# A transformer layer on one core: Ada sums beside the next part's rows, a fifth PSUM bank for the mLSTM scores, and the order of columns at the first boundary

## The chip, the cores and the metric

The kernel runs on one core of a Trainium2 chip. The metric is the device time of one execution in microseconds (us). Engines are named as in the profile: PE (TensorE, matmuls), DVE (VectorE), ACT (ScalarE), POOL (GpSimd), SP (SyncE, here only a queue of DMA issues).

## What is computed

One layer on x of 256 x 2048 in fp32, with a condition vector c of 2048 values. Cut to what matters:

```python
ada = silu(c) @ w_ada + b_ada                 # 2048 x 18432
sh1, sc1, g1, sh2, sc2, g2, sh3, sc3, g3 = split(ada, 9)
h = swiglu(modulate(x, sh1, sc1), ffn1_w_in, ffn1_w_out)
x = layernorm(ALPHA * x + 0.5 * (1 + g1) * h)
h = token_mixer(modulate(x, sh2, sc2), w_in, ..., w_out)
x = layernorm(ALPHA * x + (1 + g2) * h)
h = swiglu(modulate(x, sh3, sc3), ffn2_w_in, ffn2_w_out)
x = layernorm(ALPHA * x + 0.5 * (1 + g3) * h)
```

`modulate` is a layer norm, times 1 + scale, plus shift. The token mixer multiplies by `w_in` and runs eight heads of causal softmax attention with forget gates (fox) and four mLSTM heads (q and k through a short convolution, then for each head scores q k times a decay, times v, divided by a norm), gates the result and multiplies by `w_out`.

## The kernel before

All matmuls with weights take each fp32 weight tile apart into a high and a low part and add three products: high weight with high x, low weight with high x, high weight with low x (lines 369, 370, 371). For a weight tile `raw` that SP loads (1 MB, line 344), ACT writes `hi` (a cast, line 142) and DVE writes `lo` = raw - hi (line 143). A lo tile is named after its use: `lo_fv512_12` is the third of unit 1 of the columns fv.

The stages in time: the start (the first Ada values), the first feed-forward part, boundary 1 (layer norm, modulation, first columns of the mixer), the mixer (columns named mo, fv512, mv512, mv0, m0, m1, fb, fbk, fa, fak, fv0, with attention and mLSTM heads among them), the out-projection (`o_mx`, weights mxo), boundary 2, the second feed-forward part, the end.

**The Ada queue.** Most of `silu(c) @ w_ada` is summed in the background on DVE. A part is 1024 columns: 16 rows of 128 x 1024, each loaded by SP into `ar` (two buffers) and added as `acc += ar * silu(c)` (lines 155 and 157). A row is called ar6_0_7: vector 6, part 0, row 7. Then the part's end: the sum over the 128 partitions, by a split of acc into `ahi` and `alo`, two matmuls with ones into a bank `bc`, and either a diagonal product `dg` and a reduction (pairs of shift and scale) or an addition into `gate`. The queue is one generator. `pump(n)` adds n to what is owed (R_MX a step in the mixer) and takes that many rows; a PAUSE inside a part's end stops it until the next step, so no row of the next part stands beside the end of one. `need(n)` runs the queue on until n vectors are done. Rows are pinned: they stay on DVE where they were recorded.

**PSUM.** Eight banks: a ring `mm` of five for the large products, a ring `aux` of three for all small ones: transposes `tp`, `bc`, and for each mLSTM head `gb` (the gate row over the partitions, and the second score block), `sps` (the first score block) and `nps` (two: numerator and norm). DVE turns sps and gb into `dm` (lines 1264, 1265), PE multiplies dm with v into nps (1271), DVE makes `dn` from nps (1276 to 1279), ACT scales nps into yM (1280) and squares into nps (1281).

**Boundaries.** `boundary` modulates pairs of 128-column blocks: ACT or DVE writes the normed `n` (312), PE transposes it into tp (316), ACT and DVE write the modulated columns `xf` (326, 323), then ACT and DVE split it into `xhi`, `xlo` (332, 334). For boundary 1 there are eight pairs; the later ones are written beside the first mixer products.

What sets the order: the framework's scheduler puts each engine's instructions in order by its own estimate, except where `manual_schedule` or a pin keeps the order of the code. Every engine then takes its own queue strictly in order.

Of the kernel before, what the change touches and what calls it, by code (L numbers as in the profile page):

```python
# [7 lines left out]
F32 = mybir.dt.float32  # L8
# [6 lines left out]
P = 128  # L15
# [17 lines left out]
def layer_kernel(  # L33
# [30 lines left out]
    def mm_tile(name):  # L64
        return pm.tile([P, 512], F32, tag="mm", name=name)

# [105 lines left out]

    def ada_pair(v, js):
        for j in js:
            src = pair_cols(v, j)
            acc = ap.tile([P, 2, 512], F32, tag="acc", name=f"acc{v}_{j}")
            for k in range(KD):
                raw = ap.tile([P, 2, 512], F32, tag="araw", bufs=2, name=f"ar{v}_{j}_{k}")
                SP.dma_start(raw, src[k * P:(k + 1) * P])
                ada_acc(acc, raw, k)  # L180
                yield
            for i in range(2):
                parts = ada_split(acc[:, i, :], f"{v}_{j}_{i}")
                for _ in range(2):
                    yield PAUSE
                bc = ada_sum(parts, f"{v}_{j}_{i}")
                dg = ap.tile([P, 4, P], F32, tag="alo", name=f"dg{v}_{j}_{i}")
                V.tensor_tensor(out=dg, in0=bc.rearrange("p (a b) -> p a b", b=P),
                                in1=ident.unsqueeze(1).to_broadcast([P, 4, P]), op=ALU.mult)
                V.tensor_reduce(out=scsh[:, v + i, j * 4:(j + 1) * 4], in_=dg, axis=AX.X, op=ALU.add)  # L190
            cs = scsh[:, v:v + 2, j * 4:(j + 1) * 4]
            V.tensor_tensor(out=cs, in0=cs, in1=bcol[:, v:v + 2, j * 4:(j + 1) * 4], op=ALU.add)

    def ada_gate(v, s):
        for j in range(2):
            c0 = v * D + j * 1024
            acc = ap.tile([P, 1024], F32, tag="acc", name=f"acc{v}_{j}")
            for k in range(KD):
                raw = ap.tile([P, 1024], F32, tag="araw", bufs=2, name=f"ar{v}_{j}_{k}")
                SP.dma_start(raw, w_ada[0, k * P:(k + 1) * P, c0:c0 + 1024])  # L200
                ada_acc(acc, raw, k)
                yield
            for i in range(2):
                parts = ada_split(acc[:, i * 512:(i + 1) * 512], f"{v}_{j}_{i}")
                yield PAUSE
                if i == 0:
                    G_.dma_start(gate[:, j * 1024:(j + 1) * 1024], b_ada[0:1, c0:c0 + 1024].to_broadcast([P, 1024]))
                yield PAUSE
                bc = ada_sum(parts, f"{v}_{j}_{i}")
                gs = gate[:, j * 1024 + i * 512:j * 1024 + (i + 1) * 512]  # L210
                V.scalar_tensor_tensor(out=gs, in0=bc, scalar=1.0, in1=gs, op0=ALU.add, op1=ALU.add)
                if s != 1.0:
                    V.tensor_scalar_mul(gs, gs, s)

    ada_left = {}
    PAUSE = 1

    def ada_queue(*parts):
        def gen():
            for p in parts:  # L220
                yield from p
                parts_done[0] += 1
                yield PAUSE
        ada_left["g"] = gen()

    parts_done = [0]
    owed = [0]

    def pump(n):
        owed[0] += n  # L230
        while owed[0] >= 1:
            with pinned():
                got = next(ada_left["g"], 0)
            if got is PAUSE:
                break
            owed[0] -= 1


    def need(n):
        while parts_done[0] < n and next(ada_left["g"], 0) != 0:  # L240
            owed[0] = 0

# [30 lines left out]
    def ntag():  # L273
        seq[0] += 1
        return str(seq[0])
# [29 lines left out]
    def modulate_tile(v, a, k0, nk, rs, xT, xs=None, on_v=False):  # L305
        ts_ = slice(a * P, (a + 1) * P)
        n = npool.tile([P, nk * P], F32, tag="n", bufs=2, name=f"n_{ntag()}")
        r = res[:, a, k0 * P:(k0 + nk) * P]
        if on_v:
            V.tensor_scalar(out=n, in0=r, scalar1=rs[:, 2:3], scalar2=rs[:, 0:1], op0=ALU.add, op1=ALU.mult)  # L310
        else:
            S.activation(n, r, AF.Identity, bias=rs[:, 1:2], scale=rs[:, 0:1])
        tp = aux_tile(f"tp{ntag()}")
        tpv = tp.rearrange("p (k t) -> p k t", k=4)
        for q in range(nk):
            PE.transpose(tpv[:, q, :], n[:, q * P:(q + 1) * P], ident)
        yield
        xf = npool.tile([P, nk, P], F32, tag="xf" if xs is None else "xe", bufs=2 if xs is None else 6,
                        name=f"xf{ntag()}")
        for q in range(nk):  # L320
            k = k0 + q
            if q % 2 and (a or k0 >= 6):
                V.tensor_scalar(out=xf[:, q, :], in0=tpv[:, q, :], scalar1=scsh[:, v + 1, k:k + 1],
                                scalar2=scsh[:, v, k:k + 1], op0=ALU.mult, op1=ALU.add)
            else:
                S.activation(xf[:, q, :], tpv[:, q, :], AF.Identity,
                             bias=scsh[:, v, k:k + 1], scale=scsh[:, v + 1, k:k + 1])
# [238 lines left out]
    def boundary(add_up, st, lgb, v, tag, xT, entry, nk, raws):  # L566
# [16 lines left out]
        m = [[modulate_tile(v, a, k, 2, mr[a], xT, xs if k < 6 else None, a + k == 0) for k in range(0, nk, 2)]  # L583
             for a in range(2)]
        m0, m1 = m
# [50 lines left out]
        with tc.manual_schedule(engines={dve}):  # L636
            for i in range(3, len(m0)):
# [280 lines left out]
    gap(lnp, 320, "gap_h")  # L918
    need(1)
    W = w_in[0]  # L920
# [13 lines left out]
    def finish1(products, add_up, st):  # L934
        need(2)
        products(0)
# [33 lines left out]
    mow = {}  # L970
    fence, _, xs, ws = boundary(*ent["f"], lgb, 3, "1", xT, entry_of(mo_load, mow, 3, 6), KD, raws)
    lnp.release()

# [56 lines left out]

    def cols_form_b(c0, col, ws, use, name):
        ps = {(a, b): mm_tile(f"b_{name}{col}{a}{b}") for b in range(len(ws)) for a in range(2)}
        cb = [sum(ws[:b]) for b in range(len(ws) + 1)]
# [33 lines left out]
    def form_a_four(c0, name, before_last=lambda: None):  # L1067
        ps = [mm_tile(f"pr_{name}{i}") for i in range(2)]
        for u in range(4):
# [179 lines left out]
    def mlstm_head(o, h):  # L1249
# [122 lines left out]
    def before(k):  # L1372
        until([f"row{i}" for i in (k, k + 1)])
        if k == 2:
            need(4)

# [50 lines left out]
    guw = {}  # L1427
    fence, mr2, xs, ws = boundary(*ent["f"], lgb, 6, "2", xT, entry_of(gu_load, guw, 3, 4), 8, raws)
    lnp.release()

# [35 lines left out]
    for j in range(2, 10):  # L1466
# [3 lines left out]
        if j == 7:  # L1470
            mb = late_features(2, 5)
# [5 lines left out]
    mb = late_features(3, 6)  # L1477
    gups = {(a, g): mm_tile(f"gf{g}{a}") for a in range(2) for g in range(2)}
# [23 lines left out]
    ffn_in(W2, xT, hT, 10, "f2", at(R_B))  # L1502
    need(7)
    xp.release()
# [43 lines left out]
```

## Time and profile before

| | |
|---|---|
| time, median of 3 runs | 1933.53 us (1931.28 to 1937.57) |
| the profiled execution | 1933.74 us, its span 1932.0 us, mean granted clock 0.995 |
| PE busy | 1894.1 us, 98% of the span |
| DVE busy | 1485.9 us, 77% |
| ACT busy | 950.1 us, 49% |
| POOL busy | 56.4 us, 3% |
| chain that ended last | PE 83%, DMA 7%, DVE 6%, issue 2%, ACT 1% |
| moved by DMA | 510.92 MB, mean 264 GB/s |

A busy PE is modelled from pipelined matmuls: a row's duration covers its way through the array, and the next matmul starts before it ends. The share of idle time and what ended it are read from the windows and from the waits; a wait is put down to the instruction that, by the profile, came last.

### The profile page before, as it was taken

The page shows a single profiled execution, that of the slowest core. Times are in us where ns is not written, and L with a number is a line of the kernel's source. Part 1 is how long each engine was busy: PE and PEld are TensorE (multiplying, and loading weights), DVE is VectorE, ACT ScalarE, POOL GpSimd, SP SyncE. Part 2 cuts the span into 40 slices and gives each one's busy share as a digit, 9 for nine tenths or more (in the row PEclk, how much of TensorE's full clock was granted, in tenths as well). Part 3 has the DMA queues.
Part 4 walks back from the last instruction along what each step waited for, and adds up shares of the span by engine and source line. Part 5 has one row for each costly group of instructions (what it writes and reads, how often), then busy time and mean ns, then how long its engine had stood idle before and what let it go on. Part 6 is the DMA issues. An engine that isn't in the chain of part 4 may idle for free.

```text
span 1932.0 us, 32380 instructions
## 1 busy us (share of the span) xinstructions
PE 1894.1 (98%) x13133; PEld 1725.4 (89%) x13133; DVE 1485.9 (77%) x1847; ACT 950.1 (49%) x1359; POOL 56.4 (3%) x82
## 2 busy tenths in 40 slices
PE   6999999999999999999989999999999999999997
PEld 3999999999988887699989886999999999988886
DVE  6778988777778898878987888767766665555776
ACT  3554453443454554845655645555444444444562
POOL 1111100000000000100000000000000000000000
PEclk9999999999999999999999999999999999999999
DMA  9978969999898886488887894987776776655552
GB/s 356 377 260 316 327 217 307 312 310 316 289 340 290 290 304 219 153 305 305 301 295 242 300 307 165 308 292 255 250 255 226 263 239 197 233 184 193 196 194 90
DMA packets 283566, 510.92 MB, mean 264 GB/s; under 512 B 10866, under 2 KB 134418, under 8 KB 282392
## 3 DMA queue, kind: packets, MB, share of 16 engines
q1 hardware_dynamic: 275640, 480.53, 73.1%
q0 software_dynamic: 7776, 28.32, 4.2%
q8 instruction: 103, 1.69, 0.4%
q14 instruction: 47, 0.39, 0.1%
HBM read 506.71 MB, written 2.10 MB: 263 GB/s over the span
## 4 chain that ended last, share of the span: by engine, by line
PE 83%; DMA 7%; DVE 6%; issue 2%; ACT 1%; POOL 0%; SPq 0%; DVEq 0%; ACTq 0%; POOLq 0%
PE gu_f L370 8%; PE gu_f L369 8%; PE gu_f L371 8%; PE o_f L369 7%; PE o_f L371 7%; PE o_f L370 7%; PE s L369 4%; PE s L371 4%; PE s L370 4%; DMA ar<-in_w_ada_dram 4%; DVE acc L157 2%; PE fh L370 2%; PE fh L371 2%; PE fh L369 2%; PE fs L370 1%
## 5 line engine op out<-in xcount | busy, mean ns | idle before, releaser
L157 DVE SCALAR_TENSOR_TENSOR acc<-ar,csil,acc 128x1024 f32<-128x1024 f32 x242 | 307.9, 1273 | 93.6 <-DMA ar<-in_w_ada_dram 91.9
L370 PE MATMUL s<-xlo_f,hi_s 128*128 128x256 f32 x768 | 213.9, 278 | 1.1 <-DVE xlo_f L300 1.1
L369 PE MATMUL s<-xhi_f,hi_s 128*128 128x256 f32 x768 | 213.9, 279 | 0.2 <-ACT hT1a L859 0.2
L371 PE MATMUL s<-xhi_f,lo_s 128*128 128x256 f32 x768 | 213.7, 278 | 0.0
L371 PE MATMUL gu_f<-xhi_f,lo_f2i 128*128 128x256 f32 x768 | 212.3, 276 | 0.0
L369 PE MATMUL gu_f<-xhi_f,hi_f2i 128*128 128x256 f32 x768 | 212.3, 276 | 0.0
L370 PE MATMUL gu_f<-xlo_f,hi_f2i 128*128 128x256 f32 x768 | 212.3, 276 | 0.0
L143 DVE TENSOR_TENSOR lo_f2i<-raw_f2i,hi_f2i 128x1024 fp32r<-128x1024 f32 x96 | 117.5, 1225 | 88.6 <-ACT hi_f2i L142 88.6
L371 PE MATMUL gu_f<-xhi_f,lo_f1i 128*128 128x256 f32 x640 | 177.0, 277 | 0.0
L369 PE MATMUL gu_f<-xhi_f,hi_f1i 128*128 128x256 f32 x640 | 176.9, 276 | 0.0
L370 PE MATMUL gu_f<-xlo_f,hi_f1i 128*128 128x256 f32 x640 | 176.9, 276 | 0.0
L142 ACT CAST hi_f2i<-raw_f2i 128x1024 fp32r<-128x1024 f32 x96 | 100.8, 1050 | 135.2 <-PE gu_f L370 120.7
L142 ACT CAST hi_s<-raw_s 128x1024 fp32r<-128x1024 f32 x96 | 100.5, 1052 | 130.9 <-PE s L370 90.9
L370 PEld LDWEIGHTS s<-xlo_f,hi_s 128*128 128x128 f32 x768 | 145.6, 190 | 1.4 <-DVE xlo_f L300 1.4
L371 PEld LDWEIGHTS s<-xhi_f,lo_s 128*128 128x128 f32 x768 | 145.4, 189 | 0.0
L369 PEld LDWEIGHTS s<-xhi_f,hi_s 128*128 128x128 f32 x768 | 145.0, 189 | 0.4 <-ACT hT1a L859 0.4
L370 PEld LDWEIGHTS gu_f<-xlo_f,hi_f2i 128*128 128x128 f32 x768 | 144.2, 188 | 0.2
L369 PEld LDWEIGHTS gu_f<-xhi_f,hi_f2i 128*128 128x128 f32 x768 | 144.2, 188 | 0.2
L371 PEld LDWEIGHTS gu_f<-xhi_f,lo_f2i 128*128 128x128 f32 x768 | 144.2, 188 | 0.0
L143 DVE TENSOR_TENSOR lo_f2o<-raw_f2o,hi_f2o 128x1024 fp32r<-128x1024 f32 x86 | 105.3, 1224 | 43.3 <-ACT hi_f2o L142 43.3
L143 DVE TENSOR_TENSOR lo_s<-raw_s,hi_s 128x1024 fp32r<-128x1024 f32 x96 | 115.7, 1221 | 28.1 <-ACT hi_s L142 26.8
L369 PE MATMUL o_f<-hi_f1o,hh 128*128 128x512 f32 x336 | 132.2, 393 | 0.0
(476 smaller groups left out, 5402.4 us busy)
## 6 DMA issues: line engine op xcount, KB each, us to landing
ar<-in_w_ada_dram SPq DMA_DIRECT2D x227, 512.0 KB, 5.4
raw_f2i<-in_ffn_w_in_dram SPq DMA_DIRECT2D x48, 1024.0 KB, 5.1
raw_s<-in_ffn_w_in_dram SPq DMA_DIRECT2D x47, 1024.0 KB, 7.5
raw_f1o<-in_ffn_w_out_dram SPq DMA_DIRECT2D x44, 1024.0 KB, 7.5
raw_f2o<-in_ffn_w_out_dram SPq DMA_DIRECT2D x44, 1024.0 KB, 5.1
raw_f1i<-in_ffn_w_in_dram SPq DMA_DIRECT2D x40, 1024.0 KB, 7.4
ar<-in_w_ada_dram POOLq DMA_DIRECT2D x48, 512.0 KB, 6.8
raw_mxo<-in_w_out_dram SPq DMA_DIRECT2D x16, 1024.0 KB, 7.7
```

The source lines that it names most:

```text
L142: S.copy(hi, src)
L143: return V.tensor_tensor(out=lo, in0=src, in1=hi.bitcast(F32), op=ALU.subtract)
L157: V.scalar_tensor_tensor(out=acc, in0=raw, scalar=csil[:, k:k + 1], in1=acc, op0=ALU.mult, op1=ALU.add)
L369: PE.matmul(o, ah, bh, start=start, stop=False)
L370: PE.matmul(o, ah, bl, start=False, stop=False)
L371: PE.matmul(o, al, bh, start=False, stop=stop)
```

## The change

Three edits.

1. The Ada queue becomes a class. A part's end (`tail`) no longer stands in line with the rows: `pump` first takes one step of a waiting tail and then as many rows as are owed, so rows of the next part are added while the part before is being finished. Two parts are then alive at once, so parts sum alternately in the one tile `acc` and in a half of the tile `gate` (`low`, `high`), where that half isn't needed; `stage` says from which boundary on that is so. The gate's bias is loaded in two pieces of 512 columns instead of one of 1024, and `need` counts parts instead of vectors.
2. The ring `mm` gets four banks and a fifth tag `m5` takes the bank that is left. In most of the kernel `mm_tile` still goes round five. In the fox columns before the heads (`form_a_four`) and in fv0 it uses the four, and the mLSTM score tile `sps` goes into `m5` instead of the ring `aux`.
3. At boundary 1 the columns `xf` of pair i + 1 are written before the splits of pair i. `xf` gets four buffers instead of two, `xe` four instead of six.

```diff
-    pm = ctx.enter_context(tc.tile_pool(name="pm", bufs=5, space=PSUM))
+    pm = ctx.enter_context(tc.tile_pool(name="pm", bufs=1, space=PSUM))
...
+    def mm_tile(name, four=False):
+        turn[0] = 0 if four else turn[0] % 5 + 1
+        if turn[0] == 5:
+            return fifth_tile(name)
+        return pm.tile([P, 512], F32, tag="mm", bufs=4, name=name)
...
+        def row(self):
+            if self.rows is None:
+                if not self.units or self.stage < self.units[0][1]:
+                    return False
+                if self.units[0][0] is None and any(own for own, _ in self.tails):
+                    return False
+                where, _, rows, tail, shape, tag = self.units.pop(0)
+                acc = where() if where else ap.tile(shape, F32, tag="acc", name=f"acc{tag}")
...
+        def pump(self, n):
+            self.owed += n
+            with pinned():
+                if self.tails:
+                    self.tail()
+            while self.owed >= 1:
+                with pinned():
+                    if not self.row():
+                        break
+                self.owed -= 1
...
-        xf = npool.tile([P, nk, P], F32, tag="xf" if xs is None else "xe", bufs=2 if xs is None else 6,
-                        name=f"xf{ntag()}")
+        xf = npool.tile([P, nk, P], F32, tag="xf" if xs is None else "xe", bufs=4, name=f"xf{ntag()}")
...
+            columns(3)
+            for i in range(3, len(m0)):
                 if i == 3:
                     next(m1[2])
                     for b in (m0[2], m1[2]):
                         next(b)
+                if i + 1 < len(m0):
+                    columns(i + 1)
...
-        sps = [aux_tile(f"sps{h}")[:, :T], gb[:, T:T + P]]
+        sps = [fifth_tile(f"sps{h}")[:, :T], gb[:, T:T + P]]
...
-    ada_queue(ada_gate(2, 0.5), ada_pair(3, range(4)), ada_pair(6, range(2)), ada_gate(5, 1.0),
-              ada_pair(6, range(2, 3)), ada_pair(6, range(3, 4)), ada_gate(8, 0.5))
+    ada.gate(2, 0.5, None, high)
+    for j in range(4):
+        ada.pair(3, j)
+    ada.pair(6, 0)
+    ada.pair(6, 1, low, stage=1)
+    ada.gate(5, 1.0, None, high, stage=1)
+    ada.pair(6, 2)
+    ada.pair(6, 3, low, stage=2)
+    ada.gate(8, 0.5, high, None, stage=2)
...
-    cols_form_b(C_FV, 0, [512], use_fv, "fv")
+    cols_form_b(C_FV, 0, [512], use_fv, "fv", True)
```

Where it moves instructions, three places. PE at the third mLSTM head, before: from the numerator of the first head (nps01) on, with the products of the columns fbk behind gb2.

```order
L1271 MATMUL nps01_10508<-yM0_8718,dm0_10332 128x257
L1273 MATMUL nps01_10508<-yM0_8718,dm0_10332 128x257
L1257 MATMUL gb2_10524<-ng_8735,rowsel_8742 128x256
L1259 MATMUL gb2_10524<-o_2_9834 128x128
L369 MATMUL pr_fbk0_10444<-xhi_mx_8216,hi_fbk10_10540 128x256
L370 MATMUL pr_fbk0_10444<-xlo_mx_8217,hi_fbk10_10540 128x256
```

And PE there after the change.

```order
L1315 MATMUL nps01_10508<-yM0_8719,dm0_10354 128x257
L1317 MATMUL nps01_10508<-yM0_8719,dm0_10354 128x257
L1301 MATMUL gb2_10524<-ng_8736,rowsel_8743 128x256
L1303 MATMUL sps2_10525<-o_2_9834 128x256
L1303 MATMUL gb2_10524<-o_2_9834 128x128
L399 MATMUL pr_fbk0_10444<-xhi_mx_8217,hi_fbk10_10540 128x256
L400 MATMUL pr_fbk0_10444<-xlo_mx_8218,hi_fbk10_10540 128x256
```

The score product sps2 stood 21 products of fbk later and now stands between the two products into gb2; sps3 moved up by 3 in the same way.

DVE in the mixer's columns fv512, before: the lo tiles of units 1 and 2, with the Ada rows 6 and 7 of part 6_0.

```order
L143 TENSOR_TENSOR lo_fv512_11_8854<-raw_fv512_1_8835,hi_fv512_11_8853 128x520
L143 TENSOR_TENSOR lo_fv512_12_8870<-raw_fv512_1_8835,hi_fv512_12_8869 128x520
L143 TENSOR_TENSOR lo_fv512_13_8886<-raw_fv512_1_8835,hi_fv512_13_8885 128x520
L157 SCALAR_TENSOR_TENSOR acc6_0_8573<-ar6_0_6_8710,csil_94,acc6_0_8573 128x1024
L143 TENSOR_TENSOR lo_fv512_20_8907<-raw_fv512_2_8904,hi_fv512_20_8906 128x520
L157 SCALAR_TENSOR_TENSOR acc6_0_8573<-ar6_0_7_8832,csil_94,acc6_0_8573 128x1024
```

And DVE there after the change.

```order
L165 SCALAR_TENSOR_TENSOR acc6_0_8574<-ar6_0_6_8711,csil_94,acc6_0_8574 128x1024
L151 TENSOR_TENSOR lo_fv512_11_8855<-raw_fv512_1_8836,hi_fv512_11_8854 128x520
L165 SCALAR_TENSOR_TENSOR acc6_0_8574<-ar6_0_7_8833,csil_94,acc6_0_8574 128x1024
L151 TENSOR_TENSOR lo_fv512_12_8871<-raw_fv512_1_8836,hi_fv512_12_8870 128x520
L151 TENSOR_TENSOR lo_fv512_13_8887<-raw_fv512_1_8836,hi_fv512_13_8886 128x520
L151 TENSOR_TENSOR lo_fv512_20_8908<-raw_fv512_2_8905,hi_fv512_20_8907 128x520
```

Rows 6 and 7 moved up: row 7 stood behind five lo tiles of units 1 and 2 (lo_fv512_10 to _20) and now stands behind two, ahead of lo_fv512_12.

DVE at the end of the out-projection, before: the lo tiles of the last columns and rows 14 and 15 of part 6_2.

```order
L143 TENSOR_TENSOR lo_mxo1536_30_12319<-raw_mxo1536_3_12316,hi_mxo1536_30_12318 128x1024
L157 SCALAR_TENSOR_TENSOR acc6_2_12026<-ar6_2_14_12257,csil_94,acc6_2_12026 128x1024
L439 BN_STATS st_mx1_11737<-res_91 128x6
L157 SCALAR_TENSOR_TENSOR acc6_2_12026<-ar6_2_15_12296,csil_94,acc6_2_12026 128x1024
L143 TENSOR_TENSOR lo_mxo1536_31_12323<-raw_mxo1536_3_12316,hi_mxo1536_31_12322 128x1024
```

And DVE there after the change.

```order
L491 SCALAR_TENSOR_TENSOR res_91<-res_91,o_mx011_11741 128x512
L151 TENSOR_TENSOR lo_mxo1536_30_12320<-raw_mxo1536_3_12317,hi_mxo1536_30_12319 128x1024
L469 BN_STATS st_mx1_11737<-res_91 128x6
L151 TENSOR_TENSOR lo_mxo1536_31_12324<-raw_mxo1536_3_12317,hi_mxo1536_31_12323 128x1024
L151 TENSOR_TENSOR lo_mxo1536_10_12332<-raw_mxo1536_1_12329,hi_mxo1536_10_12331 128x1024
```

The two rows left this place: row 15 now stands six instructions ahead of lo_mxo1536_30, row 14 another six ahead of that.

More of the change, by code (lines that the diff above doesn't have):

```diff
@@ L171, in ada_sum @@
         return bc
[L173 to L180, printed above, removed]
-                yield
[L182 to L231, printed above, removed]
-            with pinned():
[L233 to L241, printed above, removed]
+    def ada_rows(acc, src, tag):
+        for k in range(KD):
+            raw = ap.tile(list(acc.shape), F32, tag="araw", bufs=2, name=f"ar{tag}_{k}")
+            SP.dma_start(raw, src[k * P:(k + 1) * P])
+            ada_acc(acc, raw, k)
+            yield
@@ new lines, in pair_tail @@
+    def pair_tail(acc, v, j):
+        for i in range(2):
+            parts = ada_split(acc[:, i, :], f"{v}_{j}_{i}")
+            for _ in range(2):
+                yield
+            bc = ada_sum(parts, f"{v}_{j}_{i}")
+            dg = ap.tile([P, 4, P], F32, tag="alo", name=f"dg{v}_{j}_{i}")
+            V.tensor_tensor(out=dg, in0=bc.rearrange("p (a b) -> p a b", b=P),
+                            in1=ident.unsqueeze(1).to_broadcast([P, 4, P]), op=ALU.mult)
+            V.tensor_reduce(out=scsh[:, v + i, j * 4:(j + 1) * 4], in_=dg, axis=AX.X, op=ALU.add)
+        cs = scsh[:, v:v + 2, j * 4:(j + 1) * 4]
+        V.tensor_tensor(out=cs, in0=cs, in1=bcol[:, v:v + 2, j * 4:(j + 1) * 4], op=ALU.add)
@@ new lines, in gate_tail @@
+    def gate_tail(acc, v, j, s):
+        c0 = v * D + j * 1024
+        for i in range(2):
+            parts = ada_split(acc[:, i * 512:(i + 1) * 512], f"{v}_{j}_{i}")
+            yield
+            gs = gate[:, j * 1024 + i * 512:j * 1024 + (i + 1) * 512]
+            G_.dma_start(gs, b_ada[0:1, c0 + i * 512:c0 + (i + 1) * 512].to_broadcast([P, 512]))
+            yield
+            bc = ada_sum(parts, f"{v}_{j}_{i}")
+            V.scalar_tensor_tensor(out=gs, in0=bc, scalar=1.0, in1=gs, op0=ALU.add, op1=ALU.add)
+            if s != 1.0:
+                V.tensor_scalar_mul(gs, gs, s)
@@ new lines, in layer_kernel, with __init__, pair, gate @@
+    class AdaQueue:
+        def __init__(self):
+            self.units, self.rows, self.tails = [], None, []
+            self.done = self.owed = self.left = self.stage = 0
+        def pair(self, v, j, where=None, stage=0):
+            self.units.append((where, stage, lambda acc: ada_rows(acc, pair_cols(v, j), f"{v}_{j}"),
+                               lambda acc: pair_tail(acc, v, j), [P, 2, 512], f"{v}_{j}"))
+        def gate(self, v, s, *where, stage=0):
+            for j in range(2):
+                cols = w_ada[0, :, v * D + j * 1024:v * D + (j + 1) * 1024]
+                self.units.append((where[j], stage, lambda acc, cols=cols, j=j: ada_rows(acc, cols, f"{v}_{j}"),
+                                   lambda acc, j=j: gate_tail(acc, v, j, s), [P, 1024], f"{v}_{j}"))
+        def tail(self):
+            if next(self.tails[0][1], 0) == 0:
+                self.tails.pop(0)
+                self.done += 1
+        def row(self):
[6 more added lines that the diff above has]
+                acc = where() if where else ap.tile(shape, F32, tag="acc", name=f"acc{tag}")
+                if len(shape) == 3 and where:
+                    acc = acc.rearrange("p (v n) -> p v n", v=2)
+                self.rows, self.tail_next, self.left = rows(acc), (where is None, tail(acc)), KD
+            next(self.rows)
+            self.left -= 1
+            if not self.left:
+                self.tails.append(self.tail_next)
+                self.rows = None
+            return True
+        def pump(self, n):
+            self.owed += n
+            with pinned():
+                if self.tails:
[5 more added lines that the diff above has]
+                self.owed -= 1
+        def need(self, n):
+            while self.done < n:
+                self.owed = 0
+                if self.tails:
+                    self.tail()
+                else:
+                    self.row()
@@ L245, in rsqrt @@
+    ada = AdaQueue()
+    pump, need = ada.pump, ada.need
     def rsqrt(dst, vv):
@@ L636, in boundary, with columns @@
         with tc.manual_schedule(engines={dve}):
-            for i in range(3, len(m0)):
+            def columns(i):
                 for _ in range(2):
@@ L1028, in layer_kernel, with cols_form_b @@
     emptied = [None]
[L1031 to L1032 removed]
+    def cols_form_b(c0, col, ws, use, name, four=False):
+        ps = {(a, b): mm_tile(f"b_{name}{col}{a}{b}", four) for b in range(len(ws)) for a in range(2)}
         cb = [sum(ws[:b]) for b in range(len(ws) + 1)]
@@ L1067, in form_a_four @@
     def form_a_four(c0, name, before_last=lambda: None):
-        ps = [mm_tile(f"pr_{name}{i}") for i in range(2)]
+        ps = [mm_tile(f"pr_{name}{i}", True) for i in range(2)]
         for u in range(4):
```

24 lines of the change are left out of this document (14 added, 10 removed).

## The prediction

> **What bounds the kernel now.** I read the page first, then the windows, then TensorE's waits, then the timelines of single places. The page (busy time, one costly group, one group of DMA issues):
>
> ```profile
> PE 1894.1 (98%) x13133; PEld 1725.4 (89%) x13133; DVE 1485.9 (77%) x1847; ACT 950.1 (49%) x1359; POOL 56.4 (3%) x82
> L157 DVE SCALAR_TENSOR_TENSOR acc<-ar,csil,acc 128x1024 f32<-128x1024 f32 x242 | 307.9, 1273 | 93.6 <-DMA ar<-in_w_ada_dram 91.9
> ar<-in_w_ada_dram SPq DMA_DIRECT2D x227, 512.0 KB, 5.4
> ```
>
> TensorE is busy in all but 1932.0 - 1894.1 = 37.9 us, and the change neither adds nor removes matmuls. So it can pay only where TensorE waits. The windows (length, then each engine's busy time, granted clock, DMA share, GB/s) say where that is:
>
> ```profile
> 840.00:875.00 35.00, 34.35 (x284) 33.94 (x283) 25.73 (x35) 15.07 (x29) 0.00 (x0) 1.00 0.90 310
> 875.00:970.00 95.00, 95.00 (x723) 89.84 (x722) 84.19 (x118) 59.51 (x95) 0.00 (x0) 1.00 0.87 299
> 970.00:976.00 6.00, 4.58 (x39) 4.33 (x38) 5.08 (x9) 2.94 (x7) 0.00 (x0) 1.00 0.87 303
> 988.60:992.00 3.40, 3.40 (x19) 3.40 (x18) 2.77 (x4) 0.78 (x1) 0.00 (x0) 0.50 0.93 340
> 1215.00:1900.00 685.00, 684.93 (x4939) 639.80 (x4938) 462.97 (x508) 335.40 (x432) 0.00 (x0) 1.00 0.69 231
> 1900.00:1932.00 32.00, 21.40 (x140) 19.41 (x138) 17.78 (x30) 0.26 (x1) 3.05 (x2) 0.87 0.19 66
> ```
>
> In the feed-forward parts (the second, 1215 to 1900, is shown) TensorE has no gap: whatever is reordered there is free while its cover holds, and the cover is VectorE's spare third (busy 462.97 of 685). The last window's 10.6 us tail is not touched. What can be touched lies in the mixer, and TensorE's waits name it:
>
> ```profile
> PE sps L1259 <- DVE dm L1265: 3.8, 2, 2.4
> PE o_mx L370 <- DVE lo_mxo L143: 1.9, 2, 1.3
> PE nps L1271 <- DVE dm L1265: 1.6, 1, 1.6
> PE tp L316 <- DVE xf L323: 0.8, 1, 0.8
> PE bc L170 <- DVE alo L143: 0.7, 1, 0.7
> PE o_mx L369 <- DVE res L461: 0.6, 1, 0.6
> PE b_mv L370 <- DVE lo_mv L143: 0.5, 1, 0.5
> PE o_mx L369 <- ACT yF L1086: 0.3, 1, 0.3
> PE sps L1259 <- ACT nps L1281: 0.2, 1, 0.2
> ```
>
> Those sum to 10.4 us. Sums are made against the profiled run (1933.74 us; its span 1932.0), 0.2 above the median of 1933.53. A difference of 0.3%, 5.8 us, is about what a measurement of this kernel can tell from no change.
>
> **The mLSTM heads (banks).** The timeline of TensorE at the three large waits, of the drain that frees the third, and of VectorE's products:
>
> ```profile
> 972.67 0.48 PE L1259 MATMUL sps<-o 128*128 128x256 f32 x1 [1.42 <-DVE dm L1265]
> 981.06 0.48 PE L1271 MATMUL nps<-yM,dm 128*128 128x257 f32 x1 [1.58 <-DVE dm L1265]
> 987.35 0.67 PE L1259 MATMUL sps<-o 128*128 128x256 f32 x2 [2.40 <-DVE dm L1265]
> 987.05 0.39 ACT L1281 ACTIVATE nps<-yM 128x256 f32<-128x256 f32 x1
> 972.53 0.28 DVE L1265 TENSOR_TENSOR dm<-gb,dm 128x128 f32<-128x128 f32 x1
> 972.73 2.35 DVE L143 TENSOR_TENSOR lo_fbk<-raw_fbk,hi_fbk 128x1024 fp32r<-128x1024 f32 x2
> 976.47 2.66 DVE L157 SCALAR_TENSOR_TENSOR acc<-ar,csil,acc 128x1024 f32<-128x1024 f32 x2 [1.39 <-DMA ar<-in_w_ada_dram]
> 979.05 1.22 DVE L143 TENSOR_TENSOR lo_fbk<-raw_fbk,hi_fbk 128x1024 fp32r<-128x1024 f32 x1
> 980.92 0.28 DVE L1265 TENSOR_TENSOR dm<-gb,dm 128x128 f32<-128x128 f32 x1
> ```
>
> The third wait is put down to dm, but dm1 had ended at 981.20. sps2 sits in the bank of nps00 in the ring of three, and scalar's read of nps00 ended at 987.05 + 0.39 = 987.44; with the 2.40 us went a second loss, the 988.60:992.00 row: clock 0.50 for 3.40 us, worth 1.7. Today's heads: 1.42 + 1.58 + 2.40 + 0.2 idle, 1.7 of clock: 7.3.
>
> After: sps has its own bank, so sps2's wait goes. What is late next, in order:
> (a) sps1 still needs dm0 (its bank is sps0's). VectorE gets there with five more Ada rows done (5 x 1.27 = 6.4) and one more lo (1.22): 7.6 us put into a stretch whose VectorE idle is 95.00 - 84.19 = 10.8 (875 to 970). Not all of that idle can be filled; I take dm0 1.0 later (ends 0 and 2.5): wait 2.4.
> (b) gb2 now waits for dm1, in place of nps01. From dm0's end (972.81) to dm1's (981.20) VectorE took 8.4: three lo, two acc, 1.39 of DMA wait, and dm1's own steps, 1.0. After, it has two lo and two acc: 2 x 1.22 + 2 x 1.27 + 1.0 = 6.0. TensorE needs 6.8 from sps1 to gb2's place (981.06 - 1.58 - 972.67). Wait 0.
> (c) nps10 takes the nps00 bank, 48 matmuls after gb2. The chain from dm1's end to that read is 987.44 - 981.20 = 6.2 now, and holds as many instructions after. TensorE is there some 6 us after gb2, about level; I take 0.3, and 0.3 for nps11's bank.
> (d) gb3 needs nps11's bank: 0.5 (ends 0 and 2).
> Sum 3.5; 3.5 - 7.3 = **-3.8** (ends -7.3, if nothing comes back, and -0.6, if dm0 is 1.5 later still and the low clock comes with it).
>
> The Trainium skill (TensorE: Matmul & The Clock Gate, Part 1) puts the drop to half clock after an idle window of about 3.4 us, in windows that run free of the kernel. Here it came after 2.40 us idle, so the measurement decides; by that rule the drop would not hang on this wait, and the sum would be 1.7 higher, 1931.8.
>
> **The first mixer stage: rows ahead of tiles.** Now two Ada rows stand in other places of VectorE's queue, and a row waits there for its transfer with the lo tiles behind it. VectorE at the two places, and TensorE at the first tile in question and at the mv tiles:
>
> ```profile
> 839.88 1.28 DVE L157 SCALAR_TENSOR_TENSOR acc<-ar,csil,acc 128x1024 f32<-128x1024 f32 x1 [1.95 <-DMA ar<-in_w_ada_dram]
> 840.11 0.28 PE L370 MATMUL b_fv<-lo_fv,xhi_mx 128*128 128x256 f32 x1
> 858.86 1.28 DVE L157 SCALAR_TENSOR_TENSOR acc<-ar,csil,acc 128x1024 f32<-128x1024 f32 x1 [2.83 <-DMA ar<-in_w_ada_dram]
> 860.97 0.39 PE L370 MATMUL b_mv<-lo_mv,xhi_mx 128*128 128x256 f32 x1 [0.54 <-DVE lo_mv L143]
> 872.12 0.70 DVE L143 TENSOR_TENSOR lo_mv<-raw_mv,hi_mv 128x520 fp32r<-128x520 f32 x1 [3.34 <-ACT hi_mv L142]
> ```
>
> Row 7 of that part is taken up at 839.88 because its transfer lands then; today lo_fv512_12 is ahead of it. After, it is behind: 839.88 + 1.20 + 0.70 = 841.8 against TensorE's need at 840.11: +1.7. At 858.86 the same happens with row 13, but a TensorE that is 1.7 late finds lo_mv512_10 nearly ready, and today's two losses there (0.7 and 0.3 by start-to-start times) fall into that. At 872 row 0 of the next part goes ahead of lo_mv512_30, whose hi comes late already (3.34); that row's transfer now goes out as soon as row 14 is done, near 865.5, and SP's queue holds raw_mv0_0 behind it. With the median of 5.4 it is there before the tile; with 9 it holds it by 3. I take 0.4. Sum 1.7 - 1.0 + 0.4 = **+1.1** (ends -0.5 and +4).
>
> **First boundary.** The columns of the next pair come before the current pair's splits, with four xf buffers. What goes is the tp wait (0.8 idle, 1.2 with the start-up behind it). What comes: scalar now does hi_mo_31 ahead of n171, which the second tp needs:
>
> ```profile
> 803.00 0.44 PE L316 MATMUL tp<-ident,n 128*128 128x128 f32 x2 [0.76 <-DVE xf L323]
> 799.50 0.60 ACT L312 ACTIVATE n<-res,mr 128x256 f32<-128x256 f32 x1
> 800.00 1.03 ACT L142 CAST hi_mo<-raw_mo 128x1024 fp32r<-128x1024 f32 x1
> 800.93 0.45 ACT L326 ACTIVATE xf<-tp,scsh 128x128 f32<-128x128 f32 x1
> ```
>
> n171 would start a hi_mo (1.03) and a column (0.45) later than at 799.50, so it ends at 801.6; TensorE comes to that tp 2.5 us, eleven 512-wide matmuls (0.23 each, below), before the 803.00 row: +1.1, plus 0.3 for n175 in the same way. Net about +0.2, which falls into the wait at 840, whose end a transfer sets: **0** (ends -1.2 and +1).
>
> **fv0 and out-projection.** TensorE at the first o_mx tiles:
>
> ```profile
> 1088.06 0.39 PE L369 MATMUL o_mx<-hi_mxo,yh 128*128 128x512 f32 x1
> 1089.22 0.39 PE L371 MATMUL o_mx<-hi_mxo,yl 128*128 128x512 f32 x1
> ```
>
> Five matmuls on is 1.16 us, 0.23 each. fv0's four outputs now lie in the four rotating banks, so the o_mx tile that waits for yF's copy (0.3 above) is the second instead of the fourth: six matmuls sooner, 1.4. **+1.3** (ends 0 and 1.4). The o_mx wait for res gets an Ada row between its two steps: **+0.6** (ends 0, 1.2). At the end rows 14 and 15 no longer stand between lo_mxo1536_30 and _31:
>
> ```profile
> 1162.48 1.28 DVE L157 SCALAR_TENSOR_TENSOR acc<-ar,csil,acc 128x1024 f32<-128x1024 f32 x1 [2.63 <-DMA ar<-in_w_ada_dram]
> 1166.75 0.50 PE L370 MATMUL o_mx<-lo_mxo,yh 128*128 128x512 f32 x1 [1.27 <-DVE lo_mxo L143]
> ```
>
> 2.63 + 2 x 1.2 = 5.0 us of VectorE leave that place, and TensorE's 1.9 idle, 2.8 by start-to-start times over the four tiles that are late, goes: **-2.8** (ends -2.8 and -1.0).
>
> Edits at nothing: the gate bias in two halves (six more transfers on POOL, 3% busy), tails beside rows in the feed-forward parts (no TensorE gap; if VectorE's slack failed there, a row, 1.3), the bc wait of 0.7, whose order is kept.
>
> Sum: -3.8 + 1.1 + 0 + 1.3 + 0.6 - 2.8 = -3.6, so 1933.7 - 3.6 = **1930.1**.
>
> **The rivals.**
> Faster: dm0 isn't late and the waits in the heads all go (-7.3), the fv tile waits as forecast but nothing at o_mx comes (0 for 1.3 and 0.6): -7.3 + 1.1 - 2.8 = -9.0, 1924.7. For: VectorE's DMA waits shrink where rows are spread evenly, 1.39 at 976. Against: the ring of three still holds nps.
> Same, by the clock: dm0 is 2.5 late, sps1's wait is 3.9 and takes the half clock with it: heads -0.6, total -0.4, 1933.3. For: 2.40 us was enough for the drop. By the rule of the Trainium skill above a wait of 3.9 is long enough as well.
> Slower: the transfers. Each row is 512 KB, 1.75 us at 299 GB/s; five brought forward are 8.7 us of transfer, and the raw tiles queue behind them on SP. The mechanism decides once the free share of 840 to 970 (35 x 0.10 + 95 x 0.13 = 15.9 us) is used up by waits in SP's queue, with lo_mv512_30 first. Then 8.7 reach TensorE and the head gain is lost: 8.7 + 1.1 + 1.3 + 0.6 - 2.8 = +8.9, 1942.6. Against it: 8.7 is under 15.9.
> That the change doesn't do what it says: only for the heads, where dm, not the bank, would be what sps2 waits for; the drain's end at 987.44 with the matmul at 987.35 (ends overlap the next start) speaks against that.
>
> **How the numbers follow.** Forecast 0.45 (its own range 1926.5 to 1934; of that 0.08 beyond -5.8); all head waits gone 0.23 (nearly all faster); half clock moves 0.15 (same); transfers 0.17 (slower, a little of it within). Faster 0.32, same 0.50, slower 0.18. The range reaches down past 1924.7 to 1923.5, and up to 1939, which leaves out most of the transfers' case.
>
> **What would show it.** Right: no sps row with over 1 us from an nps drain, no 0.50 clock near 989, no o_mx row waiting for lo_mxo near 1166; a b_fv wait of 1 to 2 us near 840; an sps wait of about 2.4 near 973. Wrong: 0.50 clock behind sps1's wait; raw_mv tiles waited for through hi_mv by more than 1 us near 873; new gaps in the feed-forward parts.

## The result and the profile after

The changed kernel takes 1929.12 us in the median of 21 runs (1925.75 to 1931.87), the kernel before 1933.53 in 21 runs beside it. The ratio is 0.9977, 95% interval 0.9969 to 0.9985: 4.4 us faster, clear of the runs' noise and under the 0.3% that the prediction called a change. The profiled execution has a span of 1925.6 us, 6.4 shorter than that of before; at 1927.28 us it is one of the faster runs of its kernel, while the other's profiled run, 1933.74, is at its median, so some 2 us of the 6.4 are the choice of executions.

The page after:

```profile
PE 1891.5 (98%) x13133; PEld 1724.6 (90%) x13133; DVE 1483.4 (77%) x1847; ACT 953.7 (50%) x1359; POOL 59.7 (3%) x88
```

TensorE's waits after; those listed lie in the mixer and at the boundaries, but for one of the two on `bc`, 0.60 us in the second feed-forward part (at 1300.41):

```profile
PE sps L1303 <- DVE dm L1309: 4.1, 1, 4.1
PE bc L178 <- DVE alo L151: 1.5, 2, 0.9
PE tp L347 <- ACT n L343: 1.5, 3, 0.8
```

Against the list of before: no o_mx, no nps, no b_mv, and one sps wait instead of three. The windows (length, busy time of each engine, granted clock, DMA share, GB/s):

```profile
840.00:875.00 35.00, 35.00 (x295) 35.00 (x294) 28.00 (x38) 16.87 (x30) 0.00 (x0) 1.00 0.95 328
970.00:974.30 4.30, 0.26 (x3) 0.06 (x1) 4.30 (x10) 2.26 (x3) 0.00 (x0) 1.00 0.92 315
974.30:980.00 5.70, 5.64 (x33) 5.59 (x34) 5.70 (x10) 1.93 (x6) 0.00 (x0) 0.70 1.01 354
1085.00:1172.00 87.00, 87.00 (x391) 71.28 (x390) 70.67 (x89) 37.23 (x58) 2.00 (x2) 1.00 0.82 288
```

The first mixer columns and the whole out-projection are without a gap. The heads have one, 4.1 us long, and a clock of 0.70 for 5.7 us behind it, which is worth 0.30 x 5.7 = 1.7. Adding up over each stage what lies between the starts of one matmul and the next beyond the usual distance for its width (0.113 us for 256 columns, 0.228 for 512) gives the time that TensorE loses there:

| stage (us) | before | after | after, second profile |
|---|---|---|---|
| 740 to 820, first boundary | 12.8 | 13.3 | 11.7 |
| 820 to 960, first mixer columns | 4.0 | 2.8 | 2.8 |
| 960 to 1080, heads | 17.3 | 15.4 | 16.4 |
| 1080 to 1180, out-projection | 8.5 | 5.3 | 5.5 |
| 1180 to 1220, second boundary | 9.1 | 8.0 | 7.7 |
| whole program | 93.4 | 87.1 | 85.7 |

What is taken for the narrower products moves a stage's figure by up to 0.8 and the differences between the kernels by about 0.5. The total falls by 6.3, the span by 6.4: what the trace shows lost is what this execution's span shows (the medians are 4.4 apart). In the changed kernel the second boundary begins ahead of 1180 (its first tp wait is at 1179.55), so 0.9 of the 5.3 belong to it: the waits at o_mx, 3.9 in the same count before, are gone. Most of the gain thus comes from the out-projection, 2 or less from the heads, where the fifth bank is.

Each profile is of one execution, and a stage moves by some 2 us from one to the next. In the variant cols_only, below, VectorE and ScalarE run the order of before at the heads and at the out-projection (their rows, buffer numbers left out, agree one by one), and yet it loses some 1.7 less at each.

### The profile page after: what moved, and what is told of

Its sections match the earlier page's. It is cut to its first block, busy times and chain, and to the rows that moved or that the text cites. A ratio compares the mean times of both kernels' runs of the same rounds, so it can differ in the third digit from the quotient of the medians.

```text
span 1925.6 us, 32413 instructions
## 1 busy us (share of the span) xinstructions
PE 1891.5 (98%) x13133; PEld 1724.6 (90%) x13133; DVE 1483.4 (77%) x1847; ACT 953.7 (50%) x1359; POOL 59.7 (3%) x88
## 4 chain that ended last, share of the span: by engine, by line
PE 84%; DVE 7%; DMA 5%; issue 2%; ACT 1%; SPq 0%; DVEq 0%; POOL 0%; ACTq 0%
PE gu_f L401 8%; PE gu_f L400 8%; PE gu_f L399 8%; PE o_f L399 6%; PE o_f L401 6%; PE o_f L400 6%; PE s L400 4%; PE s L399 4%; PE s L401 4%; DMA ar<-in_w_ada_dram 3%; PE fs L401 1%; PE fs L399 1%; PE fs L400 1%; PE o_mx L399 1%; PE o_mx L401 1%
## 5 line engine op out<-in xcount | busy, mean ns | idle before, releaser
L165 DVE SCALAR_TENSOR_TENSOR acc<-ar,csil,acc 128x1024 f32<-128x1024 f32 (+1 forms) x167 | 211.4, 1267 | 52.2 <-DMA ar<-in_w_ada_dram 51.5
L150 ACT CAST hi_s<-raw_s 128x1024 fp32r<-128x1024 f32 x96 | 100.6, 1052 | 130.3 <-PE s L400 93.4
L165 DVE SCALAR_TENSOR_TENSOR gate<-ar,csil,gate 128x1024 f32<-128x1024 f32 (+1 forms) x94 | 117.5, 1251 | 25.4 <-DMA ar<-in_w_ada_dram 25.2
```

The source lines that it names most:

```text
L150: S.copy(hi, src)
L165: V.scalar_tensor_tensor(out=acc, in0=raw, scalar=csil[:, k:k + 1], in1=acc, op0=ALU.mult, op1=ALU.add)
```

## The experiments

All were timed in five rounds beside the kernel before, the first four together and the last four together.

| kernel | median us | of before, same call | ratio | 95% interval |
|---|---|---|---|---|
| banks_only | 1931.44 | 1933.78 | 0.9991 | 0.9979 to 1.0002 |
| queue_only | 1932.26 | 1933.78 | 0.9991 | 0.9979 to 1.0004 |
| cols_only | 1933.05 | 1933.78 | 0.9998 | 0.9987 to 1.0009 |
| queue_banks | 1930.94 | 1933.78 | 0.9987 | 0.9976 to 0.9998 |
| after_again | 1928.68 | 1932.02 | 0.9977 | 0.9962 to 0.9991 |
| held_rows | 1923.88 | 1932.02 | 0.9946 | 0.9925 to 0.9967 |
| sps0_aux | 1930.64 | 1932.02 | 0.9987 | 0.9971 to 1.0002 |
| sps0_held | 1922.32 | 1932.02 | 0.9939 | 0.9917 to 0.9961 |

The first theory was that each edit pays at the places it was put down to, and that the Ada rows in VectorE's queue, not the bank, make the first head's decayed scores (`dm0`, which TensorE's sps1 waits for) late after the change. The rival gave the gain to one edit, or the lateness to something other than the rows.

**The fifth bank alone** (the kernel before with the four-bank ring, `fifth_tile` and sps in it).

> The fifth bank alone on the kernel before: Ada queue and boundary as before. If each edit pays where it was put down to (first theory), the heads gain and the rest stays: the first sps wait remains near 1.4 us with dm0 where it was, the 2.4 us wait of sps2 and the half clock behind it go, gb2 takes over up to 1.2 us of the nps wait; the o_mx waits at the out-projection (about 3.9 us by start-to-start times) and the mv waits (1.0) stay. Total -3 to -5 us, about 1929.5. If instead the Ada queue is what moved the heads (rival), the bank alone only moves the wait from sps2 to nps10, which needs the same drain, and the time stays within 1 us of 1933.5.

Measured 0.9991, an interval that includes no change. The windows of its profile, heads and out-projection:

```profile
960.00:1010.00 50.00, 50.00 (x410) 49.03 (x409) 41.42 (x69) 29.73 (x61) 0.00 (x0) 1.00 0.91 312
1085.00:1172.00 87.00, 85.10 (x384) 68.91 (x383) 76.48 (x100) 42.23 (x69) 0.59 (x1) 1.00 0.93 318
```

In the heads there is no gap at all, more than was expected: sps1's wait went with the others, at full clock, so the rival's return of the wait at nps10 didn't come. That sps1's went is not the bank's doing: TensorE reaches the first head's `gb0` at 968.40, 3.7 later than before (964.71), and dm0 ends only 0.7 later (973.55). Nor did the saving show in the time. This profile has waits that the one of before hasn't, 2.2 and 1.1 us at the fox heads behind and 1.3 each at two products of the first feed-forward part, with a half clock from 173.6 to 177.1 behind the second. VectorE and ScalarE run the order of before in both stages, so these waits are not shown to be the edit's. The out-projection keeps 1.9 us of gaps, 1.14 of it for yF:

```profile
1089.45 0.51 PE L377 MATMUL o_mx<-hi_mxo,yh 128*128 128x512 f32 x1 [1.14 <-ACT yF L1094]
```

Before it was 0.26: here the price of fv0 in four banks is seen, 0.9 us, in one execution.

**The Ada queue alone** (the class, `stage` and the counts in `need`; five banks in the ring).

> The Ada queue alone: ring of five and scores in the ring of three as before, boundary as before. First theory: rows done earlier take the o_mx waits at the out-projection (-3.9 us) and the mv waits (-1.0) away, and make dm0 later at the first head, so the first sps wait grows from 1.4 to about 3 us and the later waits on the ring stay: total -1 to -4 us, about 1931. Rival (the bank did it all): no gain, 1933.5 or up to 3 us slower, since rows ahead of lo tiles make new waits.

Measured 0.9991, inconclusive by the time as well. Its profile has an out-projection without a gap and pays elsewhere. TensorE's waits in the heads and just ahead:

```profile
966.00 0.39 PE L394 MATMUL pr_fb<-xhi_mx,lo_fb 128*128 128x256 f32 x1 [2.82 <-DVE lo_fb L143]
977.13 0.38 PE L1289 MATMUL gb<-ng,rowsel 128*128 128x256 f32 x1 [1.61 <-DVE dg L187]
979.67 1.22 PE L1291 MATMUL sps<-o 128*128 128x256 f32 x2 [2.16 <-DVE dm L1297]
992.91 0.67 PE L1291 MATMUL sps<-o 128*128 128x256 f32 x2 [0.36 <-DVE dm L1297]
```

And the out-projection's window:

```profile
1085.00:1172.00 87.00, 87.00 (x396) 71.54 (x395) 72.43 (x94) 42.56 (x68) 1.14 (x2) 1.00 0.91 310
```

That is 7.0 us of waits from 960 to 1000, all on VectorE: lo_fb, dg (the end of an Ada part, in a bank of the ring of three), dm. The waits of 1.61 and 2.16 stand so close together that the clock is 0.50 from 978.0 to 984.8. The loss from 960 to 1080 is 19.6 against 17.3 before, and in the out-projection 4.4 against 8.5. The mv waits went as expected, but 0.68 for acol at 897 and 0.97 for lo_m at 941 came in their place. So the queue gives four and takes about three; which is the first theory, with the lateness spread over more places than sps1.

**The columns alone** (xf and xe with four buffers, pair i + 1's columns first).

> The columns of the next pair first at the first boundary, alone. First theory: the tp wait on xf (0.8 us) goes and a tp wait on n of about the same size comes, because scalar does a hi tile first; 0 within 0.5 us. Rival: the boundary gains the whole 1.2 us, seen as no tp wait above 0.3 us after 800 us and no new wait near 840.

Measured 0.9998. The wait on xf (0.76) went, and this came:

```profile
803.83 0.44 PE L316 MATMUL tp<-ident,n 128*128 128x128 f32 x2 [0.99 <-ACT n L312]
```

As expected: nothing won there. At the heads sps2 waits 3.76 us, where before sps1 waited 1.42, nps01 1.58 and sps2 2.40; the order there is that of before, so this is how far one execution differs from another.

The edit was not without effect elsewhere, which nobody had expected. In cols_only VectorE's queue at fv512 has the order of the changed kernel, with row 7 ahead of lo_fv512_12; in banks_only, queue_only and queue_banks it has that of before. The two rows that move up there are moved by the third edit, through the scheduler, and not by the Ada queue.

**Queue and banks without the columns.**

> The change without the columns edit. First theory: as the changed kernel, 1929 within 1 us, with the tp wait of before near 802. If the edits work on the same waits, its gain is less than the sum of banks alone and queue alone; if they are independent, equal to it. Rival: the columns edit carries part of the gain, 1930.5 or more.

Measured 0.9987. The 1930.94 us is on the rival's side of its 1930.5, but the interval holds the changed kernel's 0.9977 as well as the sum of banks_only and queue_only, 0.9982: neither is shown. TensorE here waits 3.24 us for a lo_fb tile from 963.8 on, for which it doesn't wait in the changed kernel, and 2.2 for sps1, each with a half clock of 3.4 us behind it. In the changed kernel's order lo_fb21 stands on VectorE ahead of dg and the reduction, here behind them: the columns edit, 150 us earlier, moves the scheduler's estimates, and with them what stands around the heads. That the columns edit brings the 1.8 us between the two medians is therefore not shown; only that orders differ by it.

**The changed kernel again.**

> The changed kernel once more, beside the three variants and the kernel before. 1929 us within 1 us; one sps wait of 4 us at the first head with a half clock of about 3 us behind it, as in its first profile. If that wait came from one unlucky profile, it will be near 1.5 us here.

0.9977 again, and a wait of 4.5 us at sps1 in its profile. The first was no accident. The half clock lasts 6.8 us here, from 971.5 to 978.4, against 3.4 in the first profile.

**Rows held back.**

```diff
-    def step():
-        pump(R_MX)
+    def step(r=None):
+        pump(r or R_MX)
...
-            step()
+            step({"fb": .8, "fa": 2.04}.get(name[:2]))
```

> The changed kernel with Ada rows held back: 0.8 rows a step in the eight steps of the columns fb and fbk, 2.04 in the eight steps of fa and fak, 1.42 elsewhere, so that the same rows are done by the out-projection. First theory (VectorE's queue makes dm0 late: two rows fewer stand before dm0): dm0 is 2.5 to 4 us earlier, the sps wait falls from 4.1 to 1.5 or less, the half clock goes, o_mx waits stay away; -3 us against the changed kernel, about 1926. Rival (dm0 waits for the decay values from scalar or for a transfer, not for the rows): the sps wait stays at 3 to 4 us and the time at 1929.

1923.88, 4.8 us under the changed kernel in the same call, and 0.9946 of the kernel before. TensorE at sps1:

```profile
974.46 0.70 PE L1303 MATMUL sps<-o 128*128 128x256 f32 x2 [1.95 <-DVE dm L1309]
```

The windows behind it and in the out-projection:

```profile
974.50:978.00 3.50, 3.50 (x29) 3.45 (x30) 3.17 (x4) 1.51 (x5) 0.00 (x0) 1.00 1.04 410
1085.00:1172.00 87.00, 87.00 (x392) 71.26 (x391) 71.08 (x90) 36.84 (x56) 2.06 (x2) 1.00 0.83 287
```

The wait halved, the half clock went with it, and the out-projection stays without a gap, as was meant by taking more rows in fa and fak. But dm0 is not earlier by the profile's time: it ends at 974.61, in the changed kernel at 974.51, and TensorE comes to sps1 2.3 later (972.5 against 970.3), as it already was at fv512, ahead of the rows held back. A later TensorE would shorten the wait by itself, so the rows' part has to be read at equal arrival. sps0_aux, below, is the run for it: its rows are not held back, and its TensorE reaches gb0 0.3 us earlier than here. The rows of held_rows, then those of sps0_aux:

```profile
965.99 0.28 PE L1301 MATMUL gb<-ng,rowsel 128*128 128x256 f32 x1
974.33 0.28 DVE L1309 TENSOR_TENSOR dm<-gb,dm 128x128 f32<-128x128 f32 x1
...
965.69 0.28 PE L1301 MATMUL gb<-ng,rowsel 128*128 128x256 f32 x1
975.87 0.28 DVE L1309 TENSOR_TENSOR dm<-gb,dm 128x128 f32<-128x128 f32 x1
```

From gb0 to dm0's end it is 8.6 us with the rows held back (8.2 in sps0_held) and 10.5 without (10.8 and 11.2 in the two profiles of the changed kernel, 10.7 in queue_only; 8.1 before). Only queue_banks falls out, 8.9 without, its TensorE having been held 3.2 us by lo_fb just ahead of gb0. Two rows fewer stand ahead of dm0, and about 2 us go with them. So VectorE's queue, not the decay values, made dm0 late; that is a little less than the 2.5 to 4 that were expected, as is the fall of the wait to 1.95 and not to 1.5. The heads' loss falls from 15.4 or 16.4 to 11.4, and the time by 4.8 in the medians.

**The first head's scores back in the ring of three.**

```diff
-        sps = [fifth_tile(f"sps{h}")[:, :T], gb[:, T:T + P]]
+        sps = [(fifth_tile if h else aux_tile)(f"sps{h}")[:, :T], gb[:, T:T + P]]
```

> The changed kernel with the first head's scores back in the ring of three and the other three heads' in the fifth bank, so sps1 needs no dm0. First theory (the bank held by sps0 until dm0 is what TensorE waits for): the 4.1 us wait at sps1 goes; nps00 needs dm0 itself 6 us later and finds it done; gb2 waits for dm1 instead, 1 to 3 us, since dm1 stands 6 us behind dm0 on VectorE; half clock only if that passes 2 us. -2 us against the changed kernel, about 1927. Rival (VectorE's lateness is carried on whole): the wait of 4 us comes back at gb2 and the time stays at 1929.

A miss: 1930.64, no better than the changed kernel. sps1's wait did go, but not the time. TensorE in the heads:

```profile
973.46 0.38 PE L1301 MATMUL gb<-ng,rowsel 128*128 128x256 f32 x1 [1.35 <-DVE dg L195]
981.89 0.35 PE L1301 MATMUL gb<-ng,rowsel 128*128 128x256 f32 x1 [0.61 <-DVE dm L1309]
```

and after these 0.95 us at nps10 and 2.86 at gb3 for drains of nps, the last with a half clock behind it. With sps0 in the ring of three each later tile has to wait for one that stands a place nearer, and the lateness of VectorE is passed down it. The rival was right, with the place wrong.

**Both.**

> Both: rows held back and the first head's scores in the ring of three. First theory: no wait over 0.7 us from gb0 to nps31, full clock there; -4 to -5 us against the changed kernel, about 1924.5. Rival: as held_rows alone, since nothing is left to win by the bank once dm0 is early.

1922.32, 0.9939 of the kernel before: the fastest of all. The heads:

```profile
960.00:1010.00 50.00, 50.00 (x408) 48.98 (x407) 45.36 (x80) 34.16 (x70) 0.55 (x1) 1.00 0.85 301
```

No gap. Against held_rows it is 1.6 us less, within the noise of the two, but the 1.95 us wait is gone in the trace, with VectorE and ScalarE in the same order. The profile loses 2.4 more at the first boundary, with a wait of 2.26 there and a half clock behind it, which this edit doesn't touch. So the trace says that the place of sps0 pays once VectorE isn't late; the time doesn't show it. What the fifth bank itself is worth then isn't known either: the rows were not held back without it.

## Why the prediction was right, point by point

The forecast was 1930.1 in the range 1923.5 to 1939.0, and "the same within 0.3%" the likeliest; 1929.12 is 1.0 off. The sum is better than its terms: the heads came out about 2 to 3 worse than forecast, and the mixer columns, yF and res 2.3, 1.7 and 1.3 better. The errors offset each other in part: the profiled pair, from which the terms are read, differs by 6.4 where 3.6 was forecast, and the medians by 4.4. That the median comes within 1.0 of the forecast is partly luck.

**The heads: forecast -3.8, measured about -2 and -1 in the two profiles.** What was right: sps2's wait went with the bank, gb2 found dm1 done, nps01 waited for nothing. What failed is (a), dm0's lateness, taken as 1.0. It is VectorE's queue in front of it. The timeline of the changed kernel, VectorE's rows and last TensorE's:

```profile
964.51 1.27 DVE L165 SCALAR_TENSOR_TENSOR acc<-ar,csil,acc 128x1024 f32<-128x1024 f32 x1
965.71 1.22 DVE L151 TENSOR_TENSOR lo_fbk<-raw_fbk,hi_fbk 128x1024 fp32r<-128x1024 f32 x1
967.61 1.28 DVE L165 SCALAR_TENSOR_TENSOR acc<-ar,csil,acc 128x1024 f32<-128x1024 f32 x1 [0.69 <-DMA ar<-in_w_ada_dram]
968.81 2.35 DVE L151 TENSOR_TENSOR lo_fbk<-raw_fbk,hi_fbk 128x1024 fp32r<-128x1024 f32 x2
971.08 0.68 DVE L195 TENSOR_TENSOR dg<-bc,ident 128x512 f32<-128x512 f32 x1
971.68 1.21 DVE L151 TENSOR_TENSOR lo_fbk<-raw_fbk,hi_fbk 128x1024 fp32r<-128x1024 f32 x1
972.82 0.68 DVE L197 TENSOR_REDUCE scsh<-dg 128x4 f32<-128x512 f32 x1
...
974.23 0.28 DVE L1309 TENSOR_TENSOR dm<-gb,dm 128x128 f32<-128x128 f32 x1
...
974.36 0.70 PE L1303 MATMUL sps<-o 128*128 128x256 f32 x2 [4.10 <-DVE dm L1309]
```

dm0 ends at 974.51, against 972.81 before: 1.7 late, inside the bounds given (0 and 2.5). But TensorE comes to sps1 1.0 earlier than before, having lost less in the mixer columns, and that is added to the wait: 1.4 + 1.7 + 1.0 = 4.1. In the second profile dm0 is 0.6 later and TensorE 2.5 earlier, 1.3 of it already ahead of the mixer columns: 1.4 + 0.6 + 2.5 = 4.5. So against TensorE's own progress dm0 is 2.7 and 3.1 late, beyond the bound. The five more rows and the one more lo tile that the prediction counted ahead of dm0 are there; what it had too small is what they cost dm0, 1.0 of their 7.6 us. And it let every wait start from where TensorE stood before: what is won ahead of a wait on another engine is paid back at that wait, as far as the other engine doesn't come earlier with it. Held_rows, read against sps0_aux, showed the rows to be the cause. With a wait that long came the half clock, which the prediction had as a rival of its own with 15%: its mechanism is what happened, its time wasn't, since other terms went better. (c) and (d), 1.1 together, were nothing, and TensorE had been held up at sps1; in sps0_aux, where it wasn't, the same two places waited 0.95 and 2.86.

**The first mixer columns: forecast +1.1, measured -1.2.** The step that failed is the landing of row 7, held at 839.88. The transfer is issued when row 5 has freed its buffer, and row 5 is earlier too (it ends at 831.15 against 832.74). Row 7 after:

```profile
837.01 1.29 DVE L165 SCALAR_TENSOR_TENSOR acc<-ar,csil,acc 128x1024 f32<-128x1024 f32 x1 [1.54 <-DMA ar<-in_w_ada_dram]
```

Row 7 is taken up 2.9 us sooner, and lo_fv512_12 is done by 839, so no wait came at 840, and none at 872. Rows that are moved up in the queue move the issue of their own transfers up. The two losses at the mv tiles, 0.7 and 0.3, went as forecast, but not for the reason given, a TensorE that comes late: they are gone in all the other nine profiles, also in banks_only, whose order there is that of before. What took them away, and with it most of the -1.2, stays open.

**First boundary: forecast 0, measured a tp wait on n of 0.85 for one on xf of 0.76.** Right, with the mechanism: scalar does hi_mo_31 ahead of n171.

**fv0 and the out-projection: forecast +1.3, +0.6 and -2.8; measured -0.4, -0.7 and -2.8.** The last was right and is what the queue gives: the waits for lo_mxo are gone in all seven profiles that have the queue edit (queue_only without the banks), and cost 2.8, 1.2 and 2.5 in the three that haven't. The first exists, 0.9 with the bank alone; in the changed kernel it is hidden, since scalar writes yF's copies in one go as soon as fv0 ends:

```profile
1082.08 1.27 ACT L1130 COPY yF<-b_fv 128x512 f32<-128x512 f32 x2 [0.59 <-PE b_fv L401]
```

Before, the copies stood at 1089.25 behind softmax steps and a hi tile. The order of scalar's queue was not looked at there. The wait for res went, although the row that had been feared does stand between its two steps (at 1131.97). It went in banks_only and cols_only as well, whose order there is that of before; why is not shown.

**At nothing.** The second feed-forward part has one gap in the first profile, 0.60 for `alo` at 1300.41, ahead of a bc product, and none in the second. At the boundary the bc waits went from 0.9 (0.23 and 0.68) to 1.4 (0.48 and 0.94) in one profile and are not there in the other. The prediction's signs of being wrong thus came in two places, the half clock behind sps1 and this gap; its sign of being right near 840, a b_fv wait of 1 to 2 us, did not come.

**The clock.** Taking every gap of 1.3 us or more between matmuls in the ten profiles, from 60 us on, the granted clock was 0.50 behind or in those of 2.21, 2.26, 2.40, 2.86, 3.24, 3.76, 4.10 and 4.50, and behind the pair of 1.61 and 2.16 that stand 2.5 us apart; it stayed at 1.00 after 1.95 and all shorter ones, after 2.19, and also after the 2.82 of queue_only. One more drop, in banks_only from 173.6 to 177.1, stands behind a gap of 1.29. The drop lasts 3.4 us, and in two profiles (queue_only, after_again) twice that.

Where a gap falls decides it, and the traces show how. All changes of the granted clock in one profile lie a whole number of 3.413 us apart: before, the clock rises at 43.13 us and falls at 988.62, which is 277 times 3.413. Cut into windows on that grid, from 60 us to the tail, the clock fell behind each window at full clock in which TensorE sat idle for 2.05 us or more (2.05, 2.14, 2.19, 2.21, 2.40, 2.57, 2.77 twice and 3.06), and behind none with 1.85 or less but one. The window ahead of the drop before, then the two that share the gap of 2.82 in queue_only, then the one that banks_only's drop follows:

```profile
985.21:988.62 3.41, 1.27 (x9) 1.25 (x10) 2.79 (x8) 2.19 (x8) 0.00 (x0) 1.00 0.92 342
...
960.88:964.29 3.41, 2.30 (x21) 2.10 (x19) 3.41 (x9) 3.38 (x8) 0.00 (x0) 1.00 0.96 353
964.29:967.70 3.41, 1.70 (x14) 1.70 (x15) 3.41 (x5) 3.38 (x8) 0.55 (x1) 1.00 0.46 129
...
170.23:173.64 3.41, 2.12 (x19) 1.93 (x18) 3.41 (x5) 1.99 (x2) 0.87 (x2) 1.00 0.96 330
```

The 2.82 are 1.11 in one window and 1.71 in the next, and the 2.19 of banks_only 1.85 and 0.34, so neither reaches 2.05 in one. The exception is the last line: 1.29 idle, and then 0.9 us of products one column wide, from 172.58 to 173.50; if these count as idle it is 2.2 like the others, which is argued. The second half-clock window of queue_only and of after_again follows one with 1.7 idle at half clock. The Trainium skill (TensorE: Matmul & The Clock Gate, Part 1) has windows of about 3.4 us that run free of the kernel, and asks a whole one idle. The length of the windows, and that they don't start with the gap, agrees with the traces; that a whole one has to be idle doesn't, 2.05 us of 3.41 were enough.

## What to carry to other kernels

A ring of banks hands on the lateness of whichever engine empties it, so before giving one tile a bank of its own look at what stands in that engine's queue just ahead of the freeing instruction; here the bank showed no gain in the time with the queue as it was. Background work on an in-order queue should be paced by stage: the program was 4.8 us shorter with the same rows in all but two fewer ahead of a short step that TensorE waits for. When sums are made by stages, carry TensorE's new arrival into the next wait, since time won ahead of a wait on another engine comes back there. And where a scheduler orders the queues, an edit can move instructions in a place it doesn't name: compare the order in the single-edit runs before a move is put down to an edit.

## What was not expected of the hardware

Some 2 us of TensorE idle within one window of 3.41 us halve its clock for the next, which takes 1.7 us of work: a wait of 2.4 then costs 4.1, and one of 2.82 that is split between two windows costs nothing more. And a row's transfer moved by 1.6 us at its issue (from 832.77 to 831.17) landed 2.9 us sooner; in cols_only the same row, issued 0.4 later than before (833.18), landed 2.0 sooner, so what shortened the way is not shown.
